# Hybrid encoder block on one core: order of transfers, parts and products in the first column group

## The chip, the core and the metric

One core of a Trainium2 chip runs the whole program. The time is device microseconds of one execution, the median over runs. Engines are TensorE (PE in the profile, PEld for its weight loads), VectorE (DVE), ScalarE (ACT), GpSimd (POOL) and SyncE (SP), which here only issues transfers.

## The reference, cut

One layer of an encoder with 256 tokens (T) and 4096 channels (D). All tensors are float32. The part that the change touches is the first projection, and in it the columns `a_c` and `g_c`, which feed the convolution module:

```python
xn = rms_norm(h, norm_in_g[i])
proj = xn @ w_in[i]                       # (256 x 4096) @ (4096 x 14336)
q, k, v, z_a, a_c, g_c, z_c = jnp.split(proj, ...)
...
def conv_module(a, g, w_dw, b_dw, ln_g, ln_b, w_pw, b_pw):
    u = a * jax.nn.sigmoid(g)
    u = jnp.pad(u, ((0, 0), (CONV_K - 1, 0), (0, 0)))      # CONV_K = 31 taps
    u = lax.conv_general_dilated(u, w_dw[:, None, :], ..., feature_group_count=CONV_WIDTH) + b_dw
    u = jax.nn.silu(layer_norm(u, ln_g, ln_b))
    return u @ w_pw + b_pw
```

After that come chunked attention on q, k and v, the output product with `w_out`, and a gated embedding with `w_ple_gate` and `w_ple`.

## The kernel before, in words

**Exact products from parts.** A float32 operand is split in two parts that TensorE takes at its fast rate: a high part, which is a cast (`wh` for a weight tile, made on ScalarE, line 210), and a low part, which is what the cast left (`wl`, a subtraction on VectorE, line 211). A product is three matmuls: high times high, low of x times high of the weight, high of x times low of the weight (`add`, line 367; the accumulators are `acc`, and `acc_P` for the helpers named below).

**Tiles of a column group.** A group is two blocks of 512 output columns. For each of 32 blocks of 128 channels one weight tile `wt` of 128 x 2 x 512 (512 KB) is loaded by SP (line 397); two of them make a *pair*, so a group has 16 pairs. `wpool` holds five `wt`; a sixth transfer starts when the first of them has been split. The high and low tiles are three deep each, so a cast also waits until TensorE is through with the tile three places earlier.

**Plain pairs and pairs by seven products.** A plain pair costs 24 matmuls (2 blocks x 2 column blocks x 2 token halves x 3). A pair marked with `*` in an order string is done by seven products of sums in place of eight products, 21 matmuls; VectorE then also makes four sums of weight halves (lines 422 to 427), which are split too, and sums of x (`comb`, lines 262 to 280, split on lines 268 and 269). Four of the seven go to helper banks in `ps_tmp`, the pool that also takes the transposes, so the first such pair can only begin when the last transposes have been read out. The order of the pairs of a group is one of the strings on lines 317 to 322.

**The first group** (`glu_conv(0)`, order `first`) runs while x arrives. `first_pair` does pair 0 with hand-written order. x comes in eight chunks of 512 columns: `load_x(c)` issues the transfer (line 512), eight transposes on TensorE (line 169), four high parts on ScalarE (line 155) and four low parts on VectorE (line 156), two squares for the norm (line 496), and for chunks 4 to 7 the sums of x. It is called in `beside_first(n)`, between the two halves of pair n for n = 1 to 7; chunk c is needed by pairs 2c and 2c + 1. At n = 4 the transfers of eight small parameter arrays are recorded (lines 587 and 590), at n = 11 the norm's factor `r_x`.

**The second group** (`glu_conv(1)`, order `early`) follows. In every pair, `fill(fills)` takes that many pieces from the deque `later`; in this group they are taps of the convolution of the first group, one VectorE instruction each (line 634), 124 for a group's 512 columns.

**Who sets the order.** Each engine works through its own list in order. The lists are made by a scheduler that runs ahead of the chip, with its own idea of when a transfer arrives; `pin` keeps marked instructions of an engine in the order of the code, and `issue_after` puts a stretch of an engine's instructions behind a given one.

## Time and profile before

| | |
|---|---|
| median of 3 runs | 2049.4 us (2048.69 to 2051.0) |
| the profiled execution's own time | 2049.77 us |
| its span, first to last instruction | 2048.0 us |
| mean granted TensorE clock | 0.998 |
| TensorE, VectorE, ScalarE busy | 2025.9, 1872.1, 1174.0 us |
| moved by the transfers | 412.28 MB, 201 GB/s on average |

A row of the timeline gives the start, the busy time, the engine, the line, the operation and its tiles, the shape and a count; in brackets stands the idle time before it and what ended that. A matmul's end is modelled and overlaps the next one's start, so for TensorE the distance from start to start says more than the idle time. SPq is SyncE issuing a transfer. In a table by stretches each engine has its busy time and in brackets the number of its instructions.

### The profile page before, as it was taken

Reading aid. Unit: us, or ns where it says so; the run is one execution under the profiler, and the core shown is the slowest. Engines: PE = TensorE matmul, PEld = TensorE weight load, DVE = VectorE, ACT = ScalarE, POOL = GpSimd, SP = SyncE. Lnnn points to the kernel's source line nnn. Section 1 sums busy time; section 2 is a strip of 40 time slices with the busy share of each in tenths; the row PEclk is TensorE's granted clock in tenths of the full one; section 3 lists DMA queues with packets and bytes.
Section 4 is the critical chain, followed back from the end, with each engine's and each line's share of the span. In section 5 each row is a group of like instructions: output and inputs, shape, how many; then the busy total and the mean of one; then the engine's idle time right before and its main releaser. Section 6 shows DMA issues by size and latency. Waiting matters only on the chain.

```text
span 2048.0 us, 26002 instructions
## 1 busy us (share of the span) xinstructions
PE 2025.9 (99%) x9124; PEld 1662.3 (81%) x9124; DVE 1872.1 (91%) x2663; ACT 1174.0 (57%) x1513; POOL 11.9 (1%) x19
## 2 busy tenths in 40 slices
PE   9999999999999999999999999999999999999997
PEld 7787888887888788888888888888888888888875
DVE  6999999899887998865889999999999999999997
ACT  7655535554455536574556656676565666655565
POOL 0000000000000000000000000000000000000000
PEclk9999999999999999999999999999999999999999
DMA  8566665666666666566666666676666656666765
GB/s 284 187 184 209 192 196 172 197 197 192 185 187 196 199 185 189 177 189 196 192 211 201 198 216 194 218 234 207 216 197 209 210 186 211 197 220 206 233 211 173
DMA packets 166236, 412.28 MB, mean 201 GB/s; under 512 B 13006, under 2 KB 16222, under 8 KB 166106
## 3 DMA queue, kind: packets, MB, share of 16 engines
q1 hardware_dynamic: 165546, 409.59, 63.6%
q8 instruction: 71, 1.16, 0.2%
q10 hardware_dynamic: 560, 1.05, 0.2%
q14 instruction: 59, 0.48, 0.1%
HBM read 406.39 MB, written 4.19 MB: 200 GB/s over the span
## 4 chain that ended last, share of the span: by engine, by line
PE 84%; DVE 11%; issue 2%; DMA 2%; ACT 1%; ACTq 0%; POOLq 0%; POOL 0%; DVEq 0%
PE acc L367 55%; PE acc_P L367 14%; PE acc L224 12%; DVE wl L211 4%; DVE cv L634 4%; DMA wt<-in_w_in_dram 1%; PE tmp_ps L169 1%; DVE ul L211 1%; DMA wt<-in_w_out_dram 0%; PE tmp_ps L795 0%; ACT wh L210 0%; PE tmp_ps L780 0%; PE tmp_ps L813 0%; DMA wt<-in_w_ple_dram 0%; DVE ua L422 0%
## 5 line engine op out<-in xcount | busy, mean ns | idle before, releaser
L367 PE MATMUL acc<-wh,big_t 128*128 128x512 f32 x3646 | 1127.7, 391 | 1.4 <-DVE big_t L156 0.8
L210 ACT CAST wh<-wt 128x1024 fp32r<-128x1024 f32 (+1 forms) x737 | 718.5, 984 | 602.4 <-PE acc L367 350.2
L211 DVE TENSOR_TENSOR wl<-wt,wh 128x1024 fp32r<-128x1024 f32 (+1 forms) x737 | 828.1, 1134 | 91.7 <-ACT wh L210 86.0
L367 PEld LDWEIGHTS acc<-wh,big_t 128*128 128x128 f32 x3646 | 681.7, 188 | 143.3 <-ACT big_t L155 1.3
L367 PE MATMUL acc<-wl,big_t 128*128 128x512 f32 x1823 | 702.7, 391 | 1.8 <-DVE wl L211 1.8
L367 PEld LDWEIGHTS acc<-wl,big_t 128*128 128x128 f32 x1823 | 341.3, 188 | 77.3 <-DVE wl L211 6.7
L224 PE MATMUL acc<-wh,big_t 128*128 128x512 f32 x816 | 254.2, 392 | 0.0
L634 DVE SCALAR_TENSOR_TENSOR cv<-uT,dw,cv 128x234 f32<-128x234 f32 (+23 forms) x480 | 203.6, 462 | 0.9
L210 ACT CAST uh<-ub 128x1024 fp32r<-128x1024 f32 x116 | 122.0, 1051 | 118.7 <-DVE ub L427 102.8
L367 PE MATMUL acc_P<-uh,big_t 128*128 128x512 f32 x594 | 181.9, 392 | 0.2 <-DVE big_t L156 0.2
L224 PEld LDWEIGHTS acc<-wh,big_t 128*128 128x128 f32 x816 | 152.9, 188 | 31.2
L224 PE MATMUL acc<-wl,big_t 128*128 128x512 f32 x408 | 159.1, 390 | 0.0
L210 ACT CAST uh<-ua 128x1024 fp32r<-128x1024 f32 x116 | 122.1, 1053 | 60.5 <-DVE ua L423 55.0
L211 DVE TENSOR_TENSOR ul<-ub,uh 128x1024 fp32r<-128x1024 f32 x116 | 141.4, 1219 | 8.7 <-ACT uh L210 7.6
L211 DVE TENSOR_TENSOR ul<-ua,uh 128x1024 fp32r<-128x1024 f32 x116 | 141.2, 1218 | 0.4
L367 PEld LDWEIGHTS acc_P<-uh,big_t 128*128 128x128 f32 x594 | 109.7, 188 | 27.2 <-ACT uh L210 4.7
L367 PE MATMUL acc_P<-ul,big_t 128*128 128x512 f32 x297 | 113.6, 392 | 1.6 <-DVE ul L211 1.6
L422 DVE TENSOR_TENSOR ua<-wt 128x512 f32<-128x512 f32 x116 | 79.5, 685 | 25.1 <-DMA wt<-in_w_in_dram 19.6
L224 PEld LDWEIGHTS acc<-wl,big_t 128*128 128x128 f32 x408 | 76.7, 188 | 15.6
L423 DVE TENSOR_TENSOR ua<-wt 128x512 f32<-128x512 f32 x116 | 79.2, 683 | 2.6 <-DMA wt<-in_w_in_dram 2.5
L427 DVE TENSOR_TENSOR ub<-ub,wt 128x512 f32<-128x512 f32 x116 | 79.5, 685 | 1.0
L426 DVE TENSOR_TENSOR ub<-ua,wt 128x512 f32<-128x512 f32 x116 | 79.2, 683 | 0.2
(212 smaller groups left out, 1397.1 us busy)
## 6 DMA issues: line engine op xcount, KB each, us to landing
wt<-in_w_in_dram SPq DMA_DIRECT2D x446, 512.0 KB, 3.9
wt<-in_w_out_dram SPq DMA_DIRECT2D x128, 512.0 KB, 4.3
wt<-in_w_ple_gate_dram SPq DMA_DIRECT2D x128, 512.0 KB, 4.1
wt<-in_w_pw_dram SPq DMA_DIRECT2D x32, 512.0 KB, 4.6
hc<-in_x_dram SPq DMA_DIRECT2D x8, 512.0 KB, 5.4
wt<-in_w_ple_dram SPq DMA_DIRECT2D x8, 512.0 KB, 4.6
xin<-in_x_dram SPq DMA_DIRECT2D x7, 512.0 KB, 7.2
out_dram<-hc SPq DMA_DIRECT2D x12, 256.0 KB, 2.4
```

The source lines that it names most:

```text
L169: nc.tensor.transpose(pt[:, i * T + h * P : i * T + (h + 1) * P], src[:, h, b * P : (b + 1) * P], ident,)
L210: nc.scalar.copy(wh[:, :kc, :], wt[:, :kc, :]),
L211: nc.vector.tensor_tensor(wl[:, :kc, :], wt[:, :kc, :], wh[:, :kc, :].bitcast(F32), ALU.subtract),
L224: nc.tensor.matmul(acc, a, b[:, k, :], start=kb == 0 and kind == 0, stop=kb == kblocks - 1 and kind == 2,)
L367: nc.tensor.matmul(banks[name], a, b, start=name not in begun, stop=final and ends[name] == n and kind == 2 and not (left and name in "P2 ...
L422: plus(ua[:, 0], w0[:, 0], w0[:, 1])
L423: plus(ua[:, 1], w0[:, 1], w1[:, 1])
L426: plus(ub[:, 0], ua[:, 0], w1[:, 1])
L427: plus(ub[:, 1], ub[:, 0], w1[:, 0])
L634: nc.vector.scalar_tensor_tensor(cv[:, i, PAD - k :], uT[:, i, : T + k - PAD], dw[:, b, k : k + 1], cv[:, i, PAD - k :], ALU.mult, ALU.add,)
```

## The change

Five edits. (1) In the first group the weight transfers are pinned, and so is every transfer of x: SP then issues, for n = 1 to 7, both weight tiles of pair n and behind them chunk n of x. (2) Chunk 1's transposes stay where they are, but its eight parts are recorded later, in pair 2, between the splitting of that pair's first and second weight tile; the rest of the group's ScalarE work is put behind the last of them. (3) The order `first` has three pairs by seven products, 8, 10 and 12, in place of four, and a plain pair, 9, comes ahead of the first of them. (4) `r_x` is made at n = 12, where pair 13 stands in the new order as pair 11 did at n = 11 in the old one. (5) The second group takes three taps per pair in place of four, 48 in all; the other 16 stay in `later` for the groups that follow.

```diff
-    first = units("0 1 2 3 4 5 6 7 8* 9 10* 11 12* 14* 13 15")
+    first = units("0 1 2 3 4 5 6 7 9 8* 11 10* 13 12* 15 14")
...
-                nc.sync.dma_start(wt, two_columns(w, 2 * pair + k, col, apart))
+                loaded = nc.sync.dma_start(wt, two_columns(w, 2 * pair + k, col, apart))
+                if begin:
+                    pin(loaded)
...
             if not seven:
+                parts = [parts_of(wts[0], 2)[0]]
+                if amid and late_split:
+                    for ins in late_split.pop()():
+                        after.enter_context(tc.issue_after(ins.ins))
+                parts.append(parts_of(wts[1], 2)[0])
                 for k in range(2):
-                    add_plain(pair, n, k, *parts_of(wts[k], 2)[0])
+                    add_plain(pair, n, k, *parts[k])
                     if amid and k == 0:
                         amid(n)
...
+    late_split = []
+
+    def split_first(dst, pts):
+        for b in range(4):
+            hi, lo = split_from_psum(dst, b, pts[b // 2][b % 2], g_in[:, 4 + b : 5 + b])
+            pin(hi)
+        return [hi]
+
     def load_x(c):
...
+        pin(loaded)
         if c == 1:
-            pin(loaded)
-            transposed_split(xin, xT[-1], g_in, 4 * c, then=pin)
+            pts = [transposed(xin, blocks, then=pin) for blocks in ((0, 1), (2, 3))]
+            late_split.append(partial(split_first, xT[-1], pts))
...
-        if n == 11:
+        if n == 12:
             fill(len(later))
             pin(nc.vector.tensor_reduce(r_x, ssq_x, AX.X, ALU.add))
...
-            sg, gate = scaled_pair(w_in0, o_a + c * NB, o_g - o_a, early, r_x, 4)
+            sg, gate = scaled_pair(w_in0, o_a + c * NB, o_g - o_a, early, r_x, 3 if c == 1 else 4)
```

More of the change, by code (lines that the diff above doesn't have):

```diff
@@ L176, in transposed, with transposed_split @@
         return [pt[:, i * T : (i + 1) * T] for i in range(len(blocks))]
-    def transposed_split(src, dst, g, col0, **kw):
+    def transposed_split(src, dst, g, col0):
         for pair in range(2):
             blocks = (2 * pair, 2 * pair + 1)
-            for b, pt in zip(blocks, transposed(src, blocks, **kw)):
+            for b, pt in zip(blocks, transposed(src, blocks)):
                 split_from_psum(dst, b, pt, g[:, col0 + b : col0 + b + 1])
```

## The prediction

> **What bounds the kernel now.** I read the page first, then the table by stretches, then the timeline where TensorE is not full.

> ```profile
> span 2048.0 us, 26002 instructions
> PE 2025.9 (99%) x9124; PEld 1662.3 (81%) x9124; DVE 1872.1 (91%) x2663; ACT 1174.0 (57%) x1513; POOL 11.9 (1%) x19
> ```

> TensorE is busy for 2025.9 of 2048.0 us: it is the bound, and a change of order can win back only its pauses, some 22 us, the first and last microseconds among them. The change lies in the first 200 us:

> ```profile
> 12.00:24.00 12.00, 10.93 (x52) 8.25 (x51) 7.55 (x10) 9.62 (x20) 0.00 (x0) 1.00 1.05 384
> 57.00:68.00 11.00, 9.45 (x39) 6.51 (x38) 10.98 (x23) 5.42 (x9) 0.00 (x0) 1.00 0.37 111
> 68.00:105.00 37.00, 37.00 (x161) 29.38 (x160) 35.20 (x44) 22.79 (x26) 2.81 (x1) 1.00 0.71 224
> 136.00:192.00 56.00, 55.08 (x240) 44.13 (x239) 55.79 (x89) 28.89 (x32) 0.00 (x0) 1.00 0.63 195
> ```

> The columns are the length, then PE, PEld, DVE, ACT and POOL busy, the clock, and the share and rate of the transfers. Three places have pauses: 12 to 24 us, where the transfers are full (1.05 of the engines, 384 GB/s); 57 to 68 us, where VectorE is full (10.98 of 11.00); and the second group from 136 us on, where VectorE is full too (55.79 of 56.00). The clock is 1.00 throughout, so none of it is the clock.

> **Pair 2: the pause that the late parts and the order of transfers remove.** The first two rows are ScalarE, the next two VectorE, the last four TensorE.

> ```profile
> 18.23 1.05 ACT L210 CAST wh<-wt 128x1024 fp32r<-128x1024 f32 x1 [1.66 <-DMA wt<-in_w_in_dram]
> 19.18 0.83 ACT L155 ACTIVATE big_t<-tmp_ps,g_in 128x256 fp32r<-128x256 f32 x2
> 19.31 1.23 DVE L211 TENSOR_TENSOR wl<-wt,wh 128x1024 fp32r<-128x1024 f32 x1 [2.86 <-ACT wh L210]
> 20.45 0.87 DVE L156 SCALAR_TENSOR_TENSOR big_t<-tmp_ps,g_in,big_t 128x256 fp32r<-128x256 f32 x2
> 19.02 0.39 PE L367 MATMUL acc<-wl,big_t 128*128 128x512 f32 x1
> 19.70 0.51 PE L367 MATMUL acc<-wh,big_t 128*128 128x512 f32 x1 [0.29 <-ACT big_t L155]
> 20.99 0.50 PE L367 MATMUL acc<-wh,big_t 128*128 128x512 f32 x1 [0.78 <-DVE big_t L156]
> 21.32 0.40 PE L367 MATMUL acc<-wl,big_t 128*128 128x512 f32 x1
> ```

> Chunk 1's parts stand in both queues behind the second weight tile of pair 2, whose transfer stands behind two chunks of x; ScalarE idles 1.66 us for it. A matmul's pitch is 0.23 us (row 63.32 below: six in 1.54, the last of them 0.39 long). From 19.02 to 21.32 TensorE starts three matmuls in 2.30 us in place of 0.69: **1.6 us** lost.

> After the change this tile is the 15th entry of SP's list, at the place where before a parameter row stood, and both wait for the same landing, eight entries earlier (a row of SP's list, then two of the table of transfers, with the median us to landing):

> ```profile
> 12.72 0.33 SPq L587 DMA_DIRECT2D prm_rows<-in_conv_ln_b_dram  x1
> ```

> ```profile
> wt<-in_w_in_dram SPq DMA_DIRECT2D x446, 512.0 KB, 3.9
> ...
> gin_rows<-in_norm_in_g_dram SPq DMA_DIRECT2D x1, 16.0 KB, 1.9
> ```

> Issued at 12.7, landed 3.9 later by the median, at 16.6. The cast no longer decides: chunk 1's parts go ahead of it and need only the transposes, which end at the same 16.4 or so. ScalarE and VectorE take four turns of about 0.5 each (10.13 to 11.16 below, one block's high, low and next high), through by 19.4; the first block, which TensorE wants at 19.25, is through by 17.0. Then the cast 18.9 to 20.0 and the low part to 21.2; the second half of pair 2 wants them after twelve matmuls and eight transposes, at 23. So the pause goes wholly: **-1.6**. What is late next has 2 us to spare.

> Moved past it on SP are six small parameter transfers (8 or 16 KB), now ahead of that tile. In the row 12.00:24.00 several such were in the queue and it still moved 384 GB/s, so I cost them at nothing; the other end is the lone 16 KB transfer, 1.9 us each if they went one by one. [...]

> **Pair 5: a wait that the new order adds.** On ScalarE the changed program has, in this order, the four high parts of chunk 4, the cast of its sum of x (L268), and only then the first cast of pair 5:

> ```
> L155 big_t_389<-tmp_ps_390, tmp_ps_399   four, chunk 4
> L268 big_t_117<-comb_408                 sum of x, chunk 4
> L210 wh_444<-wt_440                      pair 5, first half
> L210 wh_448<-wt_442                      pair 5, second half
> ```

> Before, both casts of pair 5 stood ahead of chunk 4's parts. Chunk 4's transposes are in the middle of pair 4; what hangs on them is a chain across three engines (rows of their own lists):

> ```profile
> 9.49 0.60 PE L169 MATMUL tmp_ps<-ident,xin 128*128 128x128 f32 x4
> 10.13 0.47 ACT L155 ACTIVATE big_t<-tmp_ps,g_in 128x256 fp32r<-128x256 f32 x1 [1.81 <-PE tmp_ps L169]
> 10.64 0.48 DVE L156 SCALAR_TENSOR_TENSOR big_t<-tmp_ps,g_in,big_t 128x256 fp32r<-128x256 f32 x1
> 11.16 0.48 ACT L155 ACTIVATE big_t<-tmp_ps,g_in 128x256 fp32r<-128x256 f32 x1 [0.55 <-DVE big_t L156]
> 36.28 1.03 PE L169 MATMUL tmp_ps<-ident,xin 128*128 128x128 f32 x8
> 37.07 0.71 PE L367 MATMUL acc<-wh,big_t 128*128 128x512 f32 x2
> 41.25 0.68 DVE L280 TENSOR_TENSOR comb<-big_t 128x512 f32<-128x512 f32 x1
> ...
> 45.42 0.29 DVE L265 SCALAR_TENSOR_TENSOR comb<-comb 128x128 f32<-128x128 f32 x1
> 45.74 0.62 ACT L268 CAST big_t<-comb 128x512 fp32r<-128x512 f32 x1 [1.74 <-DVE comb L265]
> 46.27 0.47 ACT L155 ACTIVATE big_t<-tmp_ps,g_in 128x256 fp32r<-128x256 f32 x1
> ```

> Count from the first transpose, T. First high part at T+0.64 (9.49 to 10.13); the low part 0.51 later, the next high 0.52 after that, the fourth low part through at T+3.1; the sum 0.68, four small steps at 0.28 or 0.29, so T+4.9; L268 follows at once, and the next ScalarE instruction 0.53 behind it, T+5.4; cast 1.05, T+6.5; low part 1.23, T+7.7. TensorE is back on matmuls 0.79 after T (36.28 to 37.07), has twelve (2.7 us) of pair 4 and reaches pair 5 at T+3.5; two need only the cast, the third, wanted at T+4.0, the low part. Row 45.74 shows that ScalarE does not go round such a wait: it idles 1.74 us for VectorE, and the part behind it starts only after. The stop is 7.7 - 4.0, about **+3.6** (3.1 with every step overlapping the next by some 0.08, as back-to-back VectorE rows do; 4.0 with a semaphore's delay at each hand-over). Queued behind it on ScalarE are pair 5's second cast, two squares and pair 6's first cast; TensorE stands still too, wants them 2.7 us or more after it goes on, and they take about 1 us each, so they add nothing.

> **Pairs 8 and 9.** Before, the first helper product waits at 57 to 68 us for VectorE to empty the banks:

> ```profile
> 59.23 0.39 PE L367 MATMUL acc<-wl,big_t 128*128 128x512 f32 x1
> 60.73 0.70 PE L367 MATMUL acc_P<-wh,big_t 128*128 128x512 f32 x2 [1.11 <-DVE big_t L156]
> 61.27 0.40 PE L367 MATMUL acc_P<-wl,big_t 128*128 128x512 f32 x1
> 61.84 0.70 PE L367 MATMUL acc_P<-uh,big_t 128*128 128x512 f32 x2 [0.17 <-DVE big_t L156]
> 63.32 1.54 PE L367 MATMUL acc<-wh,big_t 128*128 128x512 f32 x6
> 65.14 0.72 PE L367 MATMUL acc<-wl,big_t 128*128 128x512 f32 x2 [0.27 <-DVE wl L211]
> ```

> Start to start, less the pitch: 1.27 at 60.73, 0.34 at 61.84, 0.43 at 65.14 and some 0.2 in shorter ones: 2.2. Pair 9, a plain one, now stands ahead: 24 matmuls, 5.4 us, in which VectorE catches up; and the stop at pair 5 gives it 3.6 more. In VectorE's new list the first low part of pair 9 is through at about T+23.4 (its cast waits for pair 6 to leave its tile, T+20.1, with two parts and the squares ahead of it). Behind it stand chunk 7's four parts (0.48 each, 0.40 apart), three sums of 0.68, seven small steps and the copies of the parameters, some 6 us by the rows above, and then pair 9's second low part, through at T+30.6 where TensorE wants it at T+30.3: +0.3. The banks are free by T+29.4; the first helper product is wanted at T+32.9. So **-2.2 + 0.3**. One pair less by seven products is three matmuls more, 3 x 0.23 = **+0.7**; it also takes four sums and two splits off VectorE, all off the path. `r_x` moves back one plain pair and stays ahead of its first use; its power on POOL (the 2.81 us of 68 to 105) has about 3 us to spare. The squares move on ScalarE, which has room (22.79 of 37).

> **Second group.** 16 taps fewer.

> ```profile
> L634 DVE SCALAR_TENSOR_TENSOR cv<-uT,dw,cv 128x234 f32<-128x234 f32 (+23 forms) x480 | 203.6, 462 | 0.9
> ```

> 16 x 0.46 = 7.4 us off a VectorE that is full for the 56 us in which TensorE idles 0.92; a stop counts some 0.2 more than its idle time, since a matmul shows 0.39 for a pitch of 0.23, so three or four stops are about 1.6. By the first of them about six pairs have gone by, six taps, 2.8 us of relief: more than any one stop. I take **-1.5** (bounds 0 and -1.7). The 16 taps run later, where there is a fill that had none left: the fourth group would have 52 taps for 64 places and now has 64. Elsewhere the lists change in places; I put that at 0, with bounds of 1 us either way, the size of this group's pauses.

> **Sum**: -1.6 + 3.6 + 0.3 - 2.2 + 0.7 - 1.5 = **-0.7**. The profiled execution took 2049.77 (2048.0 of span and 1.8 around it), 0.4 above the median of 2049.4. From the median: **2048.7**. A change under 0.2%, 4.1 us, is about what a measurement of this kernel cannot tell from none.

> **Rivals.** *Pair 5 does not stop*: TensorE comes late to pair 4 anyway, or the casts run early enough. Then -0.7 - 3.6 = -4.3, 2045.1, and with a little won in the later groups 2044.6. For it: every other edit points that way. Against: the chain starts from TensorE's own transposes, so a late TensorE does not shorten it. 0.17, all of it counted as faster.

> *VectorE's backlog stays*: the wait at the first helper product only moves to pair 9, whose low part stands behind the same parts and copies. Then the 2.2 is not won: +1.5, 2050.9. For it: 10.98 of 11.00 busy; my margin at pair 9 is already negative. Against: the 3.6 us gift. 0.20, within 0.2%.

> *The small transfers go one by one*, so it is slower: six at 1.9 us hold the tile of pair 2 until 14.1 + 11.4 + 1.4 = 26.9 (14.1 is the landing ahead, 1.4 a tile at 384 GB/s), its low part is ready at 29.2, wanted at 23.4: +5.8, in all +5.1, 2054.5. It decides from about 1.1 us each on. Against: 384 GB/s with such transfers in the queue. With later lists that go badly beside the second rival, 0.11, all slower.

> *The forecast*, one stop removed at pair 2, one added at pair 5, the rest small: 0.52, within 0.2%.

> **Numbers.** Same is 0.52 + 0.20 = 0.72, faster 0.17, slower 0.11. The range takes in the first rival, 2044.6, and at the top the second with its bounds (the second group's 1.5 not won, or a microsecond lost later), 2052.5; the third lies outside.

> **What would show it.** Right: no pause around 19 to 21 us; one of 3 to 4 us near 38 us, in which ScalarE idles ahead of L268 and a cast of `wh` follows it; helper products without a wait; VectorE below full in the second group and no stop on `wl` or `ul` there. Wrong: a first matmul of pair 5 on time; a pause of over 2 us at pair 9; ScalarE waiting past 20 us for the tile of pair 2; new stops after 190 us of more than 2 us in all.

## The result: 3 us slower

The changed kernel takes 2053.0 us in the median of 22 runs, the kernel before 2050.0 beside it: ratio 1.0016, with a 95% interval of 1.001 to 1.0023. The forecast was 2048.7, no change; the interval lies above one, and the median above the range's top, 2052.5. The profiled execution took 2052.84 us against 2049.77 of before.

The first line of the page, and the four stretches of the table by stretches that the prediction quoted (columns as there):

```profile
span 2051.0 us, 26003 instructions
...
12.00:24.00 12.00, 12.00 (x62) 9.79 (x61) 8.16 (x10) 8.70 (x16) 0.00 (x0) 1.00 0.86 280
57.00:68.00 11.00, 11.00 (x55) 8.95 (x54) 10.98 (x24) 6.42 (x11) 0.00 (x0) 1.00 0.28 82
68.00:105.00 37.00, 37.00 (x163) 30.18 (x163) 32.89 (x40) 22.05 (x25) 2.21 (x1) 1.00 0.71 225
136.00:192.00 56.00, 55.71 (x246) 45.81 (x245) 55.80 (x90) 29.25 (x33) 0.00 (x0) 1.00 0.66 198
```

All the places that the prediction named have filled up: TensorE idles 0 us in place of 1.07 and 1.55 in the first two stretches, and 0.29 in place of 0.92 in the last. The span grew all the same. The loss is in stretches that were full before:

```profile
30.00:37.00 7.00, 7.00 (x37) 5.88 (x36) 4.06 (x9) 5.72 (x16) 0.00 (x0) 1.00 1.04 382
37.00:46.00 9.00, 5.72 (x18) 4.02 (x17) 6.43 (x11) 4.80 (x8) 0.00 (x0) 0.81 0.40 131
46.00:52.00 6.00, 6.00 (x32) 5.04 (x31) 4.24 (x8) 4.80 (x10) 0.00 (x0) 1.00 0.82 275
```

The column to look at is the clock: 0.81 in the stretch of pair 5's stop, 1.00 on both sides. The timeline of that stop, two rows of ScalarE, then TensorE:

```profile
39.29 0.62 ACT L268 CAST big_t<-comb 128x512 fp32r<-128x512 f32 x1 [2.33 <-DVE comb L265]
39.81 1.99 ACT L210 CAST wh<-wt 128x1024 fp32r<-128x1024 f32 x2
...
37.77 0.39 PE L367 MATMUL acc<-wl,big_t 128*128 128x512 f32 x1
40.91 0.73 PE L367 MATMUL acc<-wh,big_t 128*128 128x512 f32 x2 [2.75 <-ACT wh L210]
42.16 0.80 PE L367 MATMUL acc<-wl,big_t 128*128 128x512 f32 x1 [0.52 <-DVE wl L211]
42.76 1.06 PE L367 MATMUL acc<-wh,big_t 128*128 128x512 f32 x2
43.61 0.63 PE L367 MATMUL acc<-wl,big_t 128*128 128x512 f32 x1
44.04 1.06 PE L367 MATMUL acc<-wh,big_t 128*128 128x512 f32 x2
44.89 0.63 PE L367 MATMUL acc<-wl,big_t 128*128 128x512 f32 x1
45.32 0.74 PE L367 MATMUL acc<-wh,big_t 128*128 128x512 f32 x2
45.90 0.39 PE L367 MATMUL acc<-wl,big_t 128*128 128x512 f32 x1
46.12 0.60 PE L169 MATMUL tmp_ps<-ident,xin 128*128 128x128 f32 x4
```

The wait is the forecast one: L268 waits for VectorE's sums, the casts stand behind it. From 37.77 to 40.91 is 3.14, less a pitch of 0.23: 2.9, and with the low part at 42.16 (0.7) and 0.1 at the second matmul 3.7 us. Behind that no row shows a wait, and yet from 42.76 to 45.32 the starts are 0.43 apart: from 42.16 to the transposes at 46.12 ten matmuls take 3.96 us, at 0.227 each it would be 2.27. So 1.7 us more went into slow matmuls.

How far each kernel is at the same work (TensorE's rows; transposes of chunk 5, the second group's end, and the end of the product behind the third stage; before, then after, for each):

```profile
42.62 0.60 PE L169 MATMUL tmp_ps<-ident,xin 128*128 128x128 f32 x4
46.12 0.60 PE L169 MATMUL tmp_ps<-ident,xin 128*128 128x128 f32 x4
...
194.23 0.38 PE L655 MATMUL tmp_ps<-ident,z 128*128 128x128 f32 x2
195.08 0.38 PE L672 MATMUL tmp_ps<-ident,z 128*128 128x128 f32 x2
...
418.19 0.38 PE L655 MATMUL tmp_ps<-ident,z 128*128 128x128 f32 x2
421.42 0.38 PE L672 MATMUL tmp_ps<-ident,z 128*128 128x128 f32 x2
```

The changed kernel is 3.5 us late at chunk 5, 0.85 at the end of the second group and 3.2 at 420 us; the profiled executions end 3.1 apart. So two things are to be explained: 5.4 us at pair 5 (3.5 and the 1.9 it was ahead until then: 1.65 won at pair 2, and 0.25 by which this execution was ahead at chunk 1's transposes already), and 2.4 us between 195 and 420 us, where the code has no edit. There the table of waits names these, before in the first two rows, after in the next three (us waited in all, times, longest):

```profile
PE acc L367 <- DVE wl L211: 0.9, 2, 0.6
PE tmp_ps L780 <- DVE z L488: 0.7, 3, 0.3
...
PE tmp_ps L797 <- DVE z L495: 1.4, 2, 1.1
PE acc L367 <- DVE wl L211: 0.7, 1, 0.7
DVE ua L429 <- DMA wt<-in_w_in_dram: 2.6, 2, 1.5
```

The first two rows are of 192 to 900 us, so the kernel before waits even less than that in this stage; the others are of 194 to 282. The last row is VectorE's own: it waits for a weight tile. And between the two groups stands a wait that was not there before, in TensorE's timeline:

```profile
108.80 0.44 PE L672 MATMUL tmp_ps<-ident,z 128*128 128x128 f32 x2 [0.64 <-DVE z L665]
```

### The profile page after: what moved, and what is told of

Read it like the earlier page. It is cut to its first block, busy times and chain, and to the rows that moved or that the text cites. A ratio compares the mean times of both kernels' runs of the same rounds, so it can differ in the third digit from the quotient of the medians.

```text
span 2051.0 us, 26003 instructions
## 1 busy us (share of the span) xinstructions
PE 2025.8 (99%) x9127; PEld 1664.9 (81%) x9127; DVE 1870.3 (91%) x2657; ACT 1172.1 (57%) x1511; POOL 11.3 (1%) x19
## 3 DMA queue, kind: packets, MB, share of 16 engines
q10 hardware_dynamic: 560, 1.05, 0.2%
## 4 chain that ended last, share of the span: by engine, by line
PE 83%; DVE 10%; DMA 3%; issue 2%; ACT 1%; POOLq 0%; POOL 0%; ACTq 0%; DVEq 0%; SPq 0%
PE acc L367 54%; PE acc_P L367 13%; PE acc L224 13%; DVE wl L211 4%; DVE cv L651 2%; DMA wt<-in_w_in_dram 2%; DVE ul L211 1%; PE tmp_ps L169 1%; DVE ub L434 0%; ACT wh L210 0%; PE tmp_ps L812 0%; PE tmp_ps L830 0%; PE tmp_ps L797 0%; DMA wt<-in_w_ple_dram 0%; DVE ub L433 0%
## 5 line engine op out<-in xcount | busy, mean ns | idle before, releaser
L367 PE MATMUL acc<-wh,big_t 128*128 128x512 f32 x3658 | 1133.5, 392 | 3.1 <-ACT wh L210 2.8
L210 ACT CAST wh<-wt 128x1024 fp32r<-128x1024 f32 (+1 forms) x737 | 718.2, 984 | 580.0 <-PE acc L367 317.5
L211 DVE TENSOR_TENSOR wl<-wt,wh 128x1024 fp32r<-128x1024 f32 (+1 forms) x737 | 829.9, 1137 | 86.5 <-ACT wh L210 82.4
L367 PEld LDWEIGHTS acc<-wh,big_t 128*128 128x128 f32 x3658 | 684.9, 188 | 145.3 <-ACT wh L210 3.4
L367 PE MATMUL acc<-wl,big_t 128*128 128x512 f32 x1829 | 707.8, 392 | 2.1 <-DVE wl L211 2.0
L367 PEld LDWEIGHTS acc<-wl,big_t 128*128 128x128 f32 x1829 | 343.2, 188 | 76.8 <-DVE wl L211 5.8
L651 DVE SCALAR_TENSOR_TENSOR cv<-uT,dw,cv 128x250 f32<-128x250 f32 (+23 forms) x480 | 201.7, 464 | 1.0
L210 ACT CAST uh<-ub 128x1024 fp32r<-128x1024 f32 x115 | 120.9, 1052 | 129.4 <-DVE ub L434 113.0
L367 PE MATMUL acc_P<-uh,big_t 128*128 128x512 f32 x588 | 179.8, 391 | 0.1
L210 ACT CAST uh<-ua 128x1024 fp32r<-128x1024 f32 x115 | 121.2, 1053 | 67.0 <-DVE ua L430 60.0
L211 DVE TENSOR_TENSOR ul<-ub,uh 128x1024 fp32r<-128x1024 f32 x115 | 140.4, 1221 | 8.8 <-ACT uh L210 7.8
L211 DVE TENSOR_TENSOR ul<-ua,uh 128x1024 fp32r<-128x1024 f32 x115 | 140.3, 1220 | 0.3 <-ACT uh L210 0.2
L367 PEld LDWEIGHTS acc_P<-uh,big_t 128*128 128x128 f32 x588 | 109.3, 188 | 25.3 <-ACT uh L210 3.2
L367 PE MATMUL acc_P<-ul,big_t 128*128 128x512 f32 x294 | 112.9, 392 | 1.5 <-DVE ul L211 1.5
## 6 DMA issues: line engine op xcount, KB each, us to landing
wt<-in_w_in_dram SPq DMA_DIRECT2D x446, 512.0 KB, 4.1
wt<-in_w_out_dram SPq DMA_DIRECT2D x128, 512.0 KB, 4.3
wt<-in_w_ple_gate_dram SPq DMA_DIRECT2D x128, 512.0 KB, 4.1
wt<-in_w_pw_dram SPq DMA_DIRECT2D x32, 512.0 KB, 4.4
hc<-in_x_dram SPq DMA_DIRECT2D x8, 512.0 KB, 4.7
wt<-in_w_ple_dram SPq DMA_DIRECT2D x8, 512.0 KB, 4.3
xin<-in_x_dram SPq DMA_DIRECT2D x7, 512.0 KB, 8.9
```

Source lines behind the costliest of these rows:

```text
L210: nc.scalar.copy(wh[:, :kc, :], wt[:, :kc, :]),
L211: nc.vector.tensor_tensor(wl[:, :kc, :], wt[:, :kc, :], wh[:, :kc, :].bitcast(F32), ALU.subtract),
L367: nc.tensor.matmul(banks[name], a, b, start=name not in begun, stop=final and ends[name] == n and kind == 2 and not (left and name in "P2 ...
L651: nc.vector.scalar_tensor_tensor(cv[:, i, PAD - k :], uT[:, i, : T + k - PAD], dw[:, b, k : k + 1], cv[:, i, PAD - k :], ALU.mult, ALU.add,)
```

## The experiments

The theory at the start: the loss is the stop at pair 5 and a clock that fell because of it; the moved taps bring the stops of the third stage. The rival: the stop is a gift that VectorE needs, and the first group's edits cause the later stops through the lists. Ratios are to the kernel before, measured beside it; one of 11 runs has an interval of about 0.0009 either way, 1.8 us, so the profile decides on places and the ratio on signs.

**Late parts.** In `load_x`, chunks 4 to 7 only record transposes; parts and sums follow behind the next plain pair's casts.

```diff
...
+                last, made_of = parts_of(wts[1], 2)
...
+                if amid and late_rest:
+                    with tc.issue_after(made_of[0].ins):
+                        late_rest.pop()()
...
```

> The changed kernel, with the parts and the sums of chunks 4 to 7 recorded behind the two casts of the next plain pair, so that ScalarE's list has pair 5's casts ahead of chunk 4's parts and ahead of the sum's cast (L268). Theory A (what the changed kernel loses is the stop at pair 5: 3.6 us of waiting and some 2 us of slow matmuls behind it): no stop of over 1 us near 38 to 41 us, no matmuls at 0.43 us behind it, and 5 us less than the changed kernel if nothing takes the stop's place: about 2048. Theory B (the time is lost at the border of the groups and in the third stage, and the stop's 3.6 us were a gift that VectorE needs): the helper products near 60 us wait again by 2 us and pair 9 with them, and the kernel gains under 2 us: 2051 to 2053.

Measured: 2049.7 us, ratio 0.9994 (0.9985 to 1.0003). The stretch of the stop, and TensorE's waits from 20 to 112 us:

```profile
37.00:46.00 9.00, 9.00 (x46) 7.52 (x45) 6.64 (x13) 8.87 (x23) 0.00 (x0) 1.00 0.76 252
...
PE acc_P L367 <- ACT uh L210: 1.5, 1, 1.5
PE tmp_ps L684 <- DVE z L677: 0.6, 1, 0.6
```

Stop and slow matmuls are gone, 5.4 us; a wait of 1.7 us start to start at the third helper product (70.0 us) has come back. Both theories hold a part: the stop is most of the loss, and it had given VectorE the time to work off its backlog.

**Zeros in the pause.** 13 matmuls of zeros between pairs 4 and 5, added to P2's sum.

```diff
+                if amid and n == 5:
+                    for _ in range(13):
+                        pin(nc.tensor.matmul(banks["P2"], idle[:, :P], idle, start=False, stop=False))
```

> The changed kernel, with 13 more matmuls of zeros by zeros added to P2's sum between pair 4 and pair 5, where TensorE waits (13 x 0.227 = 3.0 us of work in a wait of 3.1). Theory A (TensorE's clock falls because of the idle time): pair 5's first product still comes at 40.9, but the products behind it run 0.227 us apart and not 0.427, granted clock 1.00 in 41 to 46 us: 2 us less than the changed kernel, 2051. Theory B (the 0.427 us have another cause, such as waits on the parts or the loads of weights behind the wait): the distance of 0.427 us stays and the time is that of the changed kernel or a little over it, 2053.

Measured: 2049.0 us, ratio 0.9992 (0.9983 to 1.0001).

```profile
39.54 2.75 PE L415 MATMUL acc<-idle 128*128 128x512 bf16 x12
42.22 1.66 PE L367 MATMUL acc<-wh,big_t 128*128 128x512 f32 x6
43.72 0.85 PE L367 MATMUL acc<-wl,big_t 128*128 128x512 f32 x3
```

Pair 5 starts as late as before (25.5 us behind chunk 1's transposes, as in the changed kernel), and its matmuls run at 0.23 us: the slow pitch came from the idle time, not from operands. From those transposes to chunk 5's it takes 28.4 us in place of 30.8: 1.7 of clock, 0.7 because the low part was ready. By the ratios the kernel gained 4.9 us on the changed one, known to some 2. What is over these 2.4 is won further on, at places that the edit does not touch (1.9 us of it between the transposes at 421.4 and at 505.6 us, a stage that takes 82.2 us here and 84.2 in the changed kernel); why is not known.

**Pauses alone.** 99 bursts of matmuls with pauses between them, and nothing else; one execution.

```diff
...
+    for n in range(99):
+        pause, burst = (4 * n) % 9, 40 + (7 * n) % 11
...
+            pin(nc.tensor.matmul(acc, lhs, moving[n % 2], start=i == 0, stop=i == burst - 1))
+        pin(nc.scalar.copy(spare[:, :P], acc[:, :P]))
+        for _ in range(pause):
+            pin(nc.scalar.copy(spare[:, : 2 * P], idle[:, : 2 * P]))
+        pin(nc.scalar.copy(moving[(n + 1) % 2][:, :P], spare[:, :P]))
...
```

> Only TensorE and its pauses: 99 bursts of 40 to 50 matmuls of zeros (128x512), and between two bursts a pause in which ScalarE copies; 0 to 8 copies more, each length 11 times at different distances. The block itself is left out, the output is zeros. So far pauses of 3.1 and 3.3 us start to start were followed by matmuls 0.427 us apart (2 of 2), pauses of 1.4 to 1.9 us in 2 of 12. Theory A (a length decides): below some length between 1.9 and 3.1 us no pause is followed by slow matmuls, above it each is. Theory B (it goes by when the pause falls against a beat of the clock's own): the share of pauses with slow matmuls behind them rises gradually from some 1 us to some 3 us, and a pause of 1.9 us is hit in some of its 11 and not in others. By both the slow stretch is 3 to 4 us long, that is 7 to 9 matmuls and 1.5 to 2 us lost.

Two bursts behind pauses of the same length, 2.435 us start to start (timeline, then the same 4 us by the table of stretches):

```profile
691.22 5.05 PE L105 MATMUL acc<-moving,lhs 128*128 128x512 f32 x14 [2.05 <-ACT moving L109]
942.30 5.05 PE L105 MATMUL acc<-moving,lhs 128*128 128x512 f32 x21 [2.05 <-ACT moving L109]
...
691.20:695.20 4.00, 3.98 (x11) 3.13 (x11) 0.00 (x0) 0.00 (x0) 0.00 (x0) 0.57 0.00 0
942.30:946.30 4.00, 4.00 (x18) 3.31 (x19) 0.00 (x0) 0.00 (x0) 0.00 (x0) 1.00 0.00 0
```

In 5.05 us the one burst starts 14 matmuls, the other 21. Counted over all 98 pauses:

| pause, start to start, us | 1.1 | 1.6 | 2.0 | 2.4 | 2.9 | 3.3 to 3.6 | 3.7 | 4.2 | 4.6 |
|---|---|---|---|---|---|---|---|---|---|
| followed by matmuls at 0.427 us | 0 of 11 | 0 of 11 | 0 of 11 | 7 of 11 | 6 of 11 | 8 of 10 | 10 of 11 | 11 of 11 | 11 of 11 |

The first length is 1.1, once 1.4. A slow stretch cost 1.7 us in most cases, up to 3.0 behind the longest pauses, 0.1 of it the second matmul's, which every pause had; it began up to 1.9 us after the pause. So neither theory holds alone: up to 2.0 us nothing, above it a share that rises, and two pauses of the same length differed. The trace also records when the granted clock changes, and this shows the beat: 107 changes, all of them whole multiples of 3.413 us apart (to 0.003 us), though the pauses come at uneven distances. One stretch of 3.413 us at half the clock is 1.7 us lost; in the changed kernel's trace such a stretch stands from 42.15 to 45.56 us, clock 0.50. That two equal pauses differ agrees with these steps: counted on from the slow stretch that starts at 691.2 to 691.8 us (clock 0.57 in the first of the two rows by stretches), a border of two steps falls at 940.4 to 941.0 us, inside the pause ahead of 942.30, and none inside the one ahead of 691.22.

**Half the zeros.** 6 in place of 13.

> The changed kernel with 6 matmuls of zeros instead of 13 between pair 4 and pair 5: the pause falls from 3.1 to about 1.8 us start to start, its end stays where it is. Theory A (what slows the clock is a pause between 2.0 and some 3.3 us, as in the kernel with pauses alone: 0 of 33 up to 2.0 us, 7 of 11 at 2.4): no matmuls at 0.427 us behind it, 1.6 us less than the changed kernel, 2051 or less. Theory B (any pause here slows it, or the zeros of 13 worked in another way): slow matmuls at 42 to 46 us, 2053.

```profile
39.20 1.24 PE L415 MATMUL acc<-idle 128*128 128x512 bf16 x5
41.88 0.73 PE L367 MATMUL acc<-wh,big_t 128*128 128x512 f32 x2 [1.44 <-ACT wh L210]
43.13 0.50 PE L367 MATMUL acc<-wl,big_t 128*128 128x512 f32 x1 [0.53 <-DVE wl L211]
...
40.20:43.61 3.41, 1.45 (x6) 0.73 (x5) 2.47 (x4) 3.32 (x6) 0.00 (x0) 1.00 0.00 0
43.61:47.02 3.41, 3.41 (x10) 2.58 (x9) 1.83 (x2) 1.47 (x3) 0.00 (x0) 0.50 0.79 241
```

The pause is 1.82 us, and the matmuls are slow behind it: theory A falls as it was put. What it left out is the second wait: 1.59 + 0.11 + 0.70 = 2.4 us of idle time between 40.06 and 43.13 us. The kernel with fewer taps alone (below) had the same at 60.9 us, 1.68 and some 0.4 in short waits, while a pause of 1.66 with little behind it at 70.0 us in the kernel with late parts left the clock at full speed. The steps of 3.413 us, counted on from the changes in each trace, tell these cases apart. Here is the step that holds the waits and the one behind it, in the kernel with fewer taps and in the one with late parts (columns as above: TensorE's busy time stands second, the clock behind POOL):

```profile
58.69:62.10 3.41, 1.72 (x7) 0.83 (x7) 3.39 (x9) 2.35 (x5) 0.00 (x0) 1.00 0.65 242
62.10:65.51 3.41, 3.41 (x9) 2.63 (x10) 3.41 (x9) 0.89 (x1) 0.00 (x0) 0.50 0.00 0
...
68.41:71.82 3.41, 1.93 (x8) 1.24 (x7) 3.41 (x5) 2.10 (x3) 0.00 (x0) 1.00 0.49 130
71.82:75.24 3.42, 3.42 (x16) 2.82 (x16) 3.42 (x5) 0.79 (x1) 0.00 (x0) 1.00 0.78 242
```

TensorE's busy time within one step goes with the clock of the next: 1.72 us, then 0.50; 1.93 us, then 1.00. Over all twelve traces, from 20 us on, every step at full clock with under 1.47 us of busy time was followed by one at half the clock, and none with over 1.85 us was; in between both happened. In the changed kernel the step from 38.74 to 42.15 had 0.73 us (clock 0.50 behind it) and the next lowest ahead of TensorE's last products, from 502.95, 1.87 (1.00 behind it); in the kernel before the lowest of these had 2.13, from 59.26 (1.00 behind it). So 0.73, 1.45 and 1.72 us of busy time came ahead of half the clock, and none of these steps was idle throughout; the waits of 1.59 and 0.70 us fell into one of them, and so did those of 1.68 and some 0.4; and of the two pauses of 2.435 us the one split between two steps went free. The time, 2050.9 us, ratio 1.0003 (0.9995 to 1.0012), is below the changed kernel's, but not by this stretch: from chunk 1's transposes to chunk 5's it takes 30.8 us in both.

**Taps.** 64 again in the changed kernel; 48 alone in the kernel before; 64 in the one with late parts.

```diff
-            sg, gate = scaled_pair(w_in0, o_a + c * NB, o_g - o_a, early, r_x, 3 if c == 1 else 4)
+            sg, gate = scaled_pair(w_in0, o_a + c * NB, o_g - o_a, early, r_x, 4)
```

> The changed kernel with 4 taps per pair in the second group again (64 in place of 48). Theory A (the new stops at 108.8, 238 and 279 to 281 us come from the move of 16 taps, which reorders the later lists): these go, 4 to 4.5 us, and the second group's stops on wl and ul return, 1.2 us: 3 us less than the changed kernel, 2050. Theory B (they come from the first group's edits, through the lists behind them): they stay, the second group's stops return, and the time is 1 us over the changed kernel: 2054.

> The kernel before with 3 taps per pair in the second group (48 in place of 64) and nothing else. Theory A (the move of the taps brings the later stops): the second group gains 1.2 to 1.5 us and stops of 1 us at the border of the groups and 2 to 3 us in the third stage appear: 2 to 3 us slower than before, 2052. Theory B (the later stops are of the first group's making): 1.2 to 1.5 us faster than before, 2048.5.

> The changed kernel with chunk 4's to 7's parts behind pair 5's to 9's casts, and with 64 taps in the second group as before. Theory A (48 taps bring the stops near 237 and 277 us, 64 those in the second group): against the same with 48 taps the stops near 277 us go (-2.1) and up to 0.9 us comes back at 138 to 171 us: 1 us less, 2048.5. Theory B (the tap count only shuffles small stops): the same time, 2049.7, other stops.

Measured: 2051.6 us, ratio 1.0007 (0.9998 to 1.0016); 2051.0, 1.0004 (0.9995 to 1.0013); 2048.5, 0.9991 (0.9982 to 0.9999). Against their partners, in ratio, 48 taps cost 0.9, 0.4 and 0.3 thousandths: 1.8, 0.8 and 0.6 us. None of the three is resolved by itself, none has the sign of the prediction. The traces show it by place. From the second group's end to 420 us (194.23 to 418.19 above for the kernel before) the six kernels with 64 taps take 223.9 to 224.1 us; four with 48 take 225.6 to 226.3, and the one with 48 taps alone 228.6, of which 1.7 are a slow stretch of the clock at 280.55 us. The groups of VectorE in 194 to 236 us, the changed kernel first, then the same with 64 taps:

```profile
L429 DVE TENSOR_TENSOR ua<-wt 128x512 f32<-128x512 f32 x4 | 2.8, 689 | 2.6 <-DMA wt<-in_w_in_dram 2.6
L430 DVE TENSOR_TENSOR ua<-wt 128x512 f32<-128x512 f32 x3 | 2.1, 690 | 0.3 <-DMA wt<-in_w_in_dram 0.3
...
L430 DVE TENSOR_TENSOR ua<-wt 128x512 f32<-128x512 f32 x3 | 2.1, 685 | 0.0
L429 DVE TENSOR_TENSOR ua<-wt 128x512 f32<-128x512 f32 x3 | 2.1, 684 | 0.0
```

With 48 taps VectorE idles 2.9 us ahead of the sums of products by seven, for weights that have not landed; with 64 it has taps to do there (30 in these 42 us, against 22) and idles nothing. With 64 taps VectorE is busy for 42.0 of these 42 us, so what it idles it lacks later, and TensorE waits for it at the transposes near 279 us (L797 in the changed kernel). Over all kernels of the block: in the five with 48 taps VectorE idles 2.0 to 3.2 us there and TensorE waits 1.4 to 1.5 us at those transposes; in the six with 64 they are 0.4 and 0.2 at most. At the border of the groups it is the other way about: the wait on `z` near 108 us stands in all eight kernels with pair 9 ahead of pair 8 (and `r_x` at n = 12), with 48 taps or 64, and in none of the three with the old order. So theory A holds for the third stage and falls for the border. The second group gains by the taps in the old order, 1.6 us from the transposes on `z` at its start to those at its end (84.9 us with 48 taps alone, 86.4 before), but only 0.3 in the changed kernel (86.3 against 86.6) and 0.15 with late parts; and the third stage takes back more.

**Transfers and late parts of chunk 1 alone**, with the old order and 64 taps (`first` and `n == 11` as before).

> The kernel before with the transfers of x behind the weights and the second chunk's parts ahead of a cast, without the new order of the pairs and without the move of the taps. Theory A (each edit costs what its stage shows): the stop at pair 2 goes (-1.6), the one at pair 5 comes with its slow matmuls (+5.7), the waits at the helper products go because VectorE catches up meanwhile (-2.2), no stop at the border of the groups: +1.9, 2052. Theory B (the stop at the border, 1.0, comes from these two edits too): +3, 2053, with a stop of 0.8 us at the transposes near 108 us.

Measured: 2052.2 us, ratio 1.0013 (1.0004 to 1.0022). TensorE's waits from 20 to 112 us:

```profile
PE acc L367 <- ACT wh L210: 2.8, 1, 2.8
PE acc L367 <- DVE wl L211: 0.9, 2, 0.5
```

The stop and the slow matmuls are of these two edits, and no wait stands at the border: theory A. From chunk 1's transposes to the end of the second group this kernel takes 2.0 us more than the one before, and no more from there to 420 us. Which of the two edits puts pair 5's casts behind the sum of x was not tried.

**What was left.** Late parts, 64 taps, and pair 8 plain too; then the parameters' transposes at pair 9 in place of 7.

```diff
-    first = units("0 1 2 3 4 5 6 7 9 8* 11 10* 13 12* 15 14")
+    first = units("0 1 2 3 4 5 6 7 9 8 11 10* 13 12* 15 14")
...
-        if n == D // NB - 1:
+        if n == D // NB + 1:
             parameters()
```

> As the kernel with late parts and 64 taps, with pair 8 plain too: 2 of 16 pairs by seven products. Theory A (the 1.66 us wait on uh at the third helper product is VectorE's backlog, which the pause at pair 5 had covered): the wait goes (-1.7), three matmuls come (+0.7): 1 us less, 2047.5. Theory B (VectorE is behind by more than one pair): the wait moves to pair 10, and the three matmuls are lost: 0.7 us more than with three.

> The kernel with late parts, 64 taps and two pairs by seven, with the transposes of the parameters moved from pair 7 to pair 9. In that kernel TensorE waited 1.6 us at 56.9 us for a bank for them, since chunk 7's parts, now later, hold theirs longer; its wait on uh had gone. Theory A (the wait for the bank took the place of the wait on uh): the 1.6 us go and nothing follows: 2047.1, the fastest of all, 0.15% under the kernel before. Theory B (VectorE's backlog turns up at another pair): a stop of 1 us or more elsewhere between 57 and 75 us, 2048.5.

Measured: 2048.8 us, ratio 0.9993 (0.9984 to 1.0002), then 2047.2, 0.9984 (0.9975 to 0.9993). In the first the wait on `uh` went and TensorE waited 1.6 us at 56.9 us instead, between two of the parameters' transposes, so neither theory had it; the profile names nothing for this wait, and that it was for a bank is inferred. In the second it is gone too; TensorE's waits from 20 to 300 us:

```profile
PE tmp_ps L684 <- DVE z L677: 0.7, 1, 0.7
PE acc L367 <- DVE wl L211: 0.2, 1, 0.2
```

This version is faster than both kernels: by the ratios 3.3 us under the one before (1.4 to 5.1) and 6.6 under the changed one.

## Why the prediction was wrong

*Pair 2, -1.6: right.* The table of stretches has TensorE full from 12 to 24 us. The six small transfers landed 0.2 us apart (14.01 to 15.08 us), and the tile behind them at 16.38, for 16.6 in the forecast.

*Pair 5, +3.6: the wait right, its price wrong.* It was reckoned at 3.6 and is 3.7; the chain came out step by step, with L268 at T+4.9, the first product at T+6.5 and the low part at T+7.8 (T = 34.38 us). The step that failed is the one that took a stop's cost to be its length: "The clock is 1.00 throughout, so none of it is the clock" was read off a kernel whose pauses were 1.3 us at most. With 2.9 and 0.7 us the clock fell, 1.7 us more, as the zeros and the kernel of pauses show. The term was 5.4.

*Helper products, -2.2 + 0.3, three matmuls +0.7: the waits right, the size too small.* No wait over 0.2 us is left from 57 to 105 us. That the stop gives VectorE the time for it is borne out by the kernel with late parts, where a wait of 1.7 us returns. From 3.5 us late at chunk 5 the changed kernel makes up 2.7 by the second group's end, where the terms (the second group's -1.5 among them), with the border's 1.0 taken off, give 1.7.

*The second group, -1.5: near in size, by luck.* TensorE's stops there fell by 1.2, but not for the reason given. The step "16 x 0.46 = 7.4 us off a VectorE that is full" did not happen: VectorE is busy for 55.80 of 56.00 us, as before, and ahead of the readout of the group's sums it runs 66 taps in the changed kernel and 66 in the same with four per pair (66 and 69 in the old order). It seems that the scheduler put taps of later fills in the freed places, so that mainly the taps' places in the list changed. In the changed kernel the taps are worth 0.3 of the 1.2; the rest came with the first group's edits.

*The lists elsewhere, 0 with bounds of 1: wrong.* They cost 1.0 at the border of the groups (0.8 and 0.2) and 2.4 between 195 and 420 us; new stops of more than 2 us in all behind 190 us were one of the prediction's own signs of being wrong. The second is the price of the moved taps, which the prediction took to be free wherever a later fill had room. The groups of waits show what was missed: taps also cover VectorE's wait for weights. In all, edit 5 does not win 1.5 us; in three pairs of kernels it loses 0.6 to 1.8 by the ratios, and 1.3 to 2.0 by the traces up to 420 us, the slow stretch at 280.55 left aside. What makes the wait at the border is open: it comes with the new order of the pairs and the later `r_x`, which were not tried apart.

Together: -0.7 forecast, and 1.7 for the clock, 1.0 for the border and 2.4 for the third stage make +4.4; measured 3.0. Most of the rest is in what the helper products gained beyond the sum. None of the rivals named either cause: the clock behind a stop was put at nothing, the lists at nothing with bounds of 1.

## What to carry to other kernels

A stop of a busy TensorE cost more than its length here: waits of 3.7 us took 5.4, and two waits close together, 2.4 us in all, slowed the clock too, while a wait of 1.66 us with little behind it did not. Look at the granted clock and at the start-to-start distance of the matmuls after it, where no wait is named. Before work is taken from an engine that limits a stage, ask what it was covering there: spare instructions between two transfers are worth their place. A wait that one engine has may be the time in which another catches up; taking it away is worth only the difference, until the next backlog is cleared as well. And an instruction less in the code of a stage need not be one less in the engine's list there: count the list.
